# Second part's operand forms ordered behind the first products, forms at both ends of the memory, last third of the norm behind the first column's products

## The chip, the cores and the metric

The kernel runs on one core of one Trainium2 chip. The metric is the device time of one execution in microseconds (us). Before the change it was 2646.94 us, the median of 3 runs (2643.6 to 2652.96). The core has a matrix engine (PE), a vector engine (DVE), an activation engine (ACT), a general engine (POOL), and SP, which here only issues DMAs. Each engine works through its own list of instructions in order; an instruction that waits for a semaphore holds back everything behind it on that engine. PE writes into eight banks of PSUM, each 512 floats wide.

## The reference

One step of a one-layer encoder: a half-step feed-forward layer, a mixer (RWKV-7 heads beside chunk-band attention), a second half-step feed-forward layer and a last norm. The part that matters here:

```
x = x + 0.5 * (silu(rms(x, g1) @ w_gate) * (rms(x, g1) @ w_up)) @ w_down
h = rms(x, g_mix)
proj = h @ w_in                                   # 3328 columns
x = x + concat(rwkv7(proj[:, :1792]), band_attention(proj[:, 1792:])) @ w_out
x = x + 0.5 * (silu(rms(x, g2) @ v_gate) * (rms(x, g2) @ v_up)) @ v_down
y = rms(x, g_final)
```

There are 1024 prompt rows and 8 x 16 sample rows, 1152 tokens in all; the model width is 1024, the feed-forward width 2816. Everything is float32. The change touches no arithmetic: the same products, sums and roundings are made of the same numbers.

## The kernel before

**Precision.** Every matmul operand is held as a pair: `hi`, the number rounded to the engine's fast float32 form (`fp32r`), and `lo`, what the rounding left. A product is three matmuls: hi·hi, hi·lo, lo·hi. So whatever is made for PE is made twice: ACT copies the `hi`, and POOL or DVE subtracts to get the `lo`.

**Tokens and parts.** The 1152 tokens are 9 tiles of 128 rows. In the feed-forward layers they are cut in two parts (`PARTS`): part 0 is tiles 0 to 4, in two halves of 320 tokens, and part 1 is tiles 5 to 8, in two halves of 256.

**Gate and up products.** Each block of 256 feed-forward columns is multiplied in a scheme with seven products in place of eight. For this the activations of a part are turned into seven combinations, the part's *forms* `F`, made by `_x_forms` (L237): for each of four column groups `c`, PE transposes four blocks into PSUM (`ps_n`, L250), ACT copies three of them as `hi` (L260) and DVE makes their `lo` (L261); ACT copies the fourth block into a buffer `bs` (L263), DVE makes four differences there (L262), ACT rounds all four at once (L268) and POOL makes their `lo` at once (L269). The weights get seven forms as well (`_w_forms`: DMA into `raw`, combinations `cmb` on DVE L289, `hi` on ACT L283, `lo` on POOL L284, buffers `frm`). `_gate_up` then runs, for the gate weights and for the up weights, a pass of 7 forms x 2 parts x 12 matmuls = 168 products (L325 to L327) into the tiles `pa` and `pb`, which ACT and DVE empty (`r` L332, `y` L338). There are 11 blocks, so 22 passes in each feed-forward layer.

**Down products.** `_down` reads the hidden values back from memory (`hr`, L398), makes `h` of them (hi on ACT L401, lo on POOL L402), loads and splits two rows of blocks of the down weights (`raw` L380, `spl` L162 on ACT and L163 on POOL), multiplies (`pd`, L418 to L420) and adds to the tiles `x` (L422), 11 times over.

**Mixer.** After the first layer's last down step the norm of the mixer runs in three groups of three tiles (`_norm_t`: `xn` L203, transposes L209, `xg` hi on ACT L211 and lo on DVE L212). Then `_project` loads the old state (`st`, DMA L449, transposed by PE as `ps_st`, L451) and multiplies column by column of `w_in` (`ps_p`, L225 to L227), 24 products for each of the three groups. Near the end the output projection runs tile by tile (`ps_wo`, L1229 to L1231, added to `x` in L1235), and each finished tile is normalised for the second feed-forward layer (L1412 to L1414).

**What sets the order.** The program is written in one order, and a list scheduler puts each engine's instructions in an order of its own that respects data, buffers and the written order as a priority. Buffers come from pools: a pool takes its memory at the left or the right end of SBUF and can only be opened where the memory of closed pools is free; a tag with `bufs=n` has n buffers in turn, and whoever wants the next one waits for its last reader. In the gate and up passes PSUM has two tags of four banks, `a` and `bc`.

Five places are spoken of below, named by letters:

- **A**, the start: norm of the first layer, forms of both parts, first gate pass.
- **B**, the step from the first layer's last up pass to its first down step.
- **C**, the step from its last down step to the first column of `w_in`.
- **D**, the output projection with the second layer's forms and its first gate pass.
- **E**, the step from the second layer's last up pass to its first down step.

Of the kernel before, what the change touches and what calls it, by code (L numbers as in the profile page):

```python
# [16 lines left out]
P = 128  # L17
DM = 1024
# [43 lines left out]
def _bank(k, name):  # L62
    return k.psum.tile([P, 512], F32, tag=k.ptag, name=name)
# [131 lines left out]
def _norm_t(k, v0, rooms):  # L195

    nc = k.nc
    for g in range(3):
        xns = []
        for i in range(3 * g, 3 * g + 3):  # L200
            xn = next(rooms)
            rs = _rms(k, k.x[i], xn)
            nc.vector.tensor_scalar(xn, k.x[i], rs, None, ALU.mult)  # L203
            xns.append(xn)
        hi, lo = _xg_tile(k), _xg_tile(k)
        for c in range(KC):
            ps = k.psum.tile([P, 512], F32, tag="g", name="ps_n")
            for j in range(3):
                nc.tensor.transpose(ps[:, j * P:(j + 1) * P], xns[j][:, c * P:(c + 1) * P], k.ident)  # L209
            gain = k.vec[:, v0 + c:v0 + c + 1]  # L210
            nc.scalar.activation(hi[:, c], ps[:, :TG], AF.Copy, scale=gain)  # L211
            nc.vector.scalar_tensor_tensor(  # L212
                lo[:, c], ps[:, :TG], gain, hi[:, c].bitcast(F32), ALU.mult, ALU.subtract)
        k.xg.append((hi, lo))
        yield
# [19 lines left out]
def _x_forms(k, part, xns):  # L235


    nc = k.nc
    o, n = PARTS[part]
    F = k.F[part]  # L240

    def turned(c, half):
        ps = _bank(k, "ps_n")
        t = o + half * n
        end = t + n
        while t < end:
            i, r = divmod(t, P)
            m = min(P - r, end - t)
            at = t - o - half * n
            nc.tensor.transpose(ps[:, at:at + m], xns[i - o // P][r:r + m, c * P:c * P + P],  # L250
                                k.ident[r:r + m, r:r + m])
            t += m
        return ps[:, :n]

    for c in range(4):
        buf = k.bsp.tile([P, k.bsw], F32, tag=k.bst, bufs=k.nbs, name="bs")
        bs = buf[:, :4 * n].rearrange("p (j n) -> p j n", n=n)
        x11, x12, x21, x22 = [turned(cc, half) for cc, half in ((c, 0), (c, 1), (c + 4, 0), (c + 4, 1))]
        for j, ps in enumerate((x11, x21, x22)):
            nc.scalar.activation(F[:, 0, j, c], ps, AF.Copy)  # L260
            nc.vector.tensor_tensor(F[:, 1, j, c], ps, F[:, 0, j, c].bitcast(F32), ALU.subtract)  # L261
        sub = lambda out, x, y: nc.vector.tensor_tensor(bs[:, out], x, y, ALU.subtract)  # L262
        nc.scalar.activation(bs[:, 2], x12, AF.Copy)  # L263
# [4 lines left out]
        nc.scalar.activation(F[:, 0, 3:7, c], bs, AF.Copy)  # L268
        nc.gpsimd.tensor_tensor(F[:, 1, 3:7, c], bs, F[:, 0, 3:7, c].bitcast(F32), ALU.subtract)  # L269

# [32 lines left out]
def _gate_up(k, wg, wu, hd, m, begun=None):  # L303
# [3 lines left out]
    for up, w in enumerate((wg, wu)):  # L307
        forms = begun if begun and not up else list(_w_forms(k, w[:, 2 * m * P:2 * m * P + 2 * P]))
        state = [{}, {}]
        turns = [(t, p) for t in range(7) for p in range(2)]  # L310
        if m == 0 or (up and m == NF // 2 - 1):
            turns = [(t, p) for p in range(2) for t in range(7)]
        for t, p in turns:
            frm, j, bank = forms[t]
# [3 lines left out]
            if new:  # L318
                ps = k.psum.tile([P, 512], F32, tag="a" if bank == "a" else "bc", bufs=4, name="pa" if bank == "a" else "pb")
                st[bank] = ps[:, :n]  # L320
            ps = st[bank]
            F = k.F[p]
            for c in range(4):
                kw = dict(skip_group_check=True)
                nc.tensor.matmul(ps, frm[:, 0, c], F[:, 0, j, c], start=new and c == 0, stop=False, **kw)  # L325
                nc.tensor.matmul(ps, frm[:, 0, c], F[:, 1, j, c], start=False, stop=False, **kw)  # L326
                nc.tensor.matmul(ps, frm[:, 1, c], F[:, 0, j, c], start=False, stop=c == 3, **kw)  # L327
# [7 lines left out]
            def whole(r, f, half):  # L335
                h = hs[p][:, f, half]
                y = k.hx.tile([P, k.ny], F32, tag="y", bufs=2, name="y")[:, :n]
# [34 lines left out]
def _gate_up_pool(k, s, pool):  # L372
    k.hx = pool(s, "hx")
    k.w = pool(s, "wa")
    k.psum, k.ptag = pool(s, "psum_a", space=PSUM, bufs=4), "a"


def _down_w(k, wd, f, pool, n):
    raw = k.w.tile([P, DM], F32, tag="raw", bufs=k.nraw, name="raw")
    k.nc.sync.dma_start(raw, wd[f * P:(f + 1) * P, :])  # L380
    d = pool.tile([P, 2, DM], F32R, tag="spl", bufs=n, name="spl")
    _split(k, d, raw)
    return d


def _down(k, s, pool, wd, hd, xd, done, beside=(), then=None):


# [3 lines left out]
    w2 = pool(s, "wb")  # L392
    k.h = pool(s, "hb")
    k.xp = pool(s, "xb")
    k.psum, k.ptag = pool(s, "psum_b", space=PSUM, bufs=8), "g"
    for m in range(NF // 2):
        raw = k.h.tile([P, 2, T], F32, tag="hr", bufs=1, name="hr")
        nc.sync.dma_start(raw, hd[m])  # L398
        h = k.h.tile([P, 2, 2, T], F32R, tag="h", bufs=2, name="h")
# [3 lines left out]
        d = [_down_w(k, wd, 2 * m, k.w, 3), _down_w(k, wd, 2 * m + 1, w2, 2)]  # L403
        if m == 0:
            k.x = [k.xp.tile([P, DM], F32, tag=f"x{i}", name="x") for i in range(NT)]
            for i in range(NT):
                nc.sync.dma_start(k.x[i], xd[i])
# [4 lines left out]
        for i in range(NT):  # L412
            a = slice(i * P, (i + 1) * P)
            for n in range(2):
                b = slice(512 * n, 512 * n + 512)
                ps = k.psum.tile([P, 512], F32, tag="g", name="pd")
# [824 lines left out]
def tile_encoder_step(ctx: ExitStack, tc: tile.TileContext, *aps):  # L1241
# [35 lines left out]
    with ExitStack() as s_rw, ExitStack() as s_xg:  # L1277
# [3 lines left out]
        with ExitStack() as s:  # L1281
            fp = [pool(s, f"f{p}") for p in range(2)]
            k.F = [fp[p].tile([P, 2, 7, 4, n], F32R, name="F") for p, (o, n) in enumerate(PARTS)]
            k.ny = 4 * PARTS[0][1]
            _gate_up_pool(k, s, pool)
            k.bsp, k.bst, k.nbs, k.bsw = k.hx, "y", 2, k.ny
            _constants(k, a)
            gain = _gain(k, a["norm_ff1"][0], k.hx, "hs1")
            for p, tiles in enumerate((range(5), range(5, 9))):
                xns = []  # L1290
                for i in tiles:
# [6 lines left out]
                _x_forms(k, p, xns)  # L1298
            for m in range(NF // 2):
                _gate_up(k, w[0], w[1], hd, m)  # L1300
        k.xgp = pool(s_xg, "xg1", "right")
        k.w = pool(s_xg, "w2", "right")
        k.nraw, k.spl = 2, (k.w, 3)
        with ExitStack() as s:
# [3 lines left out]
            def rooms():  # L1308
                t = k.h.tile([P, 2 * 2 * T], F32, tag="h", bufs=2, name="xn")
                for j in range(4):  # L1310
                    yield t[:, j * DM:(j + 1) * DM]
                t = k.h.tile([P, 2 * T], F32, tag="hr", bufs=1, name="xn")
                for j in range(2):
                    yield t[:, j * DM:(j + 1) * DM]
                t = k.h.tile([P, 2 * 2 * T], F32, tag="h", bufs=2, name="xn")
                for j in range(4):
                    yield t[:, j * DM:(j + 1) * DM]

            def done(i):
# [9 lines left out]
            next(norm)  # L1329
            k.first = [_cols(k, a["w_in"][0], c * P) for c in (12, 13)]  # L1330
# [6 lines left out]
        k.psum = pool(s_xg, "psum_g", space=PSUM, side="right", bufs=5)  # L1337
        k.iv = pool(s_xg, "iv", "right")
# [36 lines left out]
    with ExitStack() as s:  # L1375
        fp = [pool(s, "f0")]
        k.F = [fp[0].tile([P, 2, 7, 4, PARTS[0][1]], F32R, name="F")]
        k.hx = pool(s, "hx")
        k.ny = DM
        with ExitStack() as sx:  # L1380
# [4 lines left out]
            k.psum, k.ptag = pool(s_ps, "psum3", space=PSUM, bufs=8), "g"  # L1385
# [14 lines left out]
            for i in range(NT):  # L1400
# [19 lines left out]
            fp.append(pool(s, "f1", "right"))  # L1420
            k.F.append(fp[1].tile([P, 2, 7, 4, PARTS[1][1]], F32R, name="F"))
            k.bsp, k.nbs, k.bsw = pool(s, "bs2", "right"), 2, 4 * PARTS[1][1]
        k.w = pool(s, "wa")
        forms = list(_w_forms(k, w[0][:, 0:2 * P]))
        _x_forms(k, 1, xns[5:])
        s_ps.close()
        k.psum, k.ptag = pool(s, "psum_a", space=PSUM, bufs=4), "a"
        for m in range(NF // 2):
            _gate_up(k, w[0], w[1], hd, m, forms if m == 0 else None)
    with ExitStack() as s:  # L1430
# [9 lines left out]
        k.w = pool(s, "w4")  # L1440
        gp = pool(s, "gain", "right")
# [34 lines left out]
```

## Time and profile before

| what | value |
|---|---|
| median of 3 runs | 2646.94 us |
| the profiled execution's own time | 2648.95 us |
| its span, first to last instruction | 2647.2 us |
| mean granted PE clock | 0.958 |
| DVE busy | 1113.4 us (42%) |
| ACT busy | 900.9 us (34%) |
| POOL busy | 1086.7 us (41%) |
| DMA, mean over the span | 108 GB/s |

The page says how long each engine was busy. The view of waits sums, for each line of the program, the time in which the engine stood still before it and what ended that time. The timeline gives single instructions: start, duration, engine, line, what is written and what is read, how many alike follow each other, and in brackets the idle time before them with its releaser. `SPq` and `ACTq` are DMAs issued from those engines' queues.

### The profile page before, as it was taken

The numbers are of one execution on the slowest core, as the hardware profiler recorded it, in microseconds if no ns is written. First come the engines' busy times: TensorE is split into PE (matmuls) and PEld (weight loads), VectorE is DVE, ScalarE is ACT, GpSimd is POOL, SyncE is SP. The second block draws the span as 40 slices with busy tenths as digits, with TensorE's granted clock in tenths as the row PEclk, the third lists the DMA queues.
The fourth block names the chain that finished last, engine by engine and source line by source line (L and its number), as shares of the span: only waits on it lengthen the run. The fifth ranks groups of instructions, "written<-read, shape, count | busy, mean of one in ns | idle before, by whom it ended". The sixth has DMA issues, their size and how long they took to land. (4 is left out here: it accounts for less than half of the span.)

```text
span 2647.2 us, 43489 instructions
## 1 busy us (share of the span) xinstructions
PE 2429.4 (92%) x17415; PEld 2165.0 (82%) x17415; DVE 1113.4 (42%) x2330; ACT 900.9 (34%) x1903; POOL 1086.7 (41%) x966
## 2 busy tenths in 40 slices
PE   3999999978999899999997999987999999979998
PEld 2999999976888799889875666666999999968886
DVE  5322222213545533856845656344322222225555
ACT  4433333321111443444214667423333333321112
POOL 4645454443443233443224443123554545544341
PEclk9999999998999899999996879988999999989999
DMA  3222112237322223543669983512221122252221
GB/s 111 66 66 84 59 59 84 66 106 243 109 84 68 98 67 125 168 141 113 191 141 205 229 181 99 181 56 72 66 74 62 65 84 66 69 202 81 93 94 72
DMA packets 230283, 284.75 MB, mean 108 GB/s; under 512 B 54920, under 2 KB 183552, under 8 KB 227264
## 3 DMA queue, kind: packets, MB, share of 16 engines
q1 hardware_dynamic: 194044, 226.72, 27.7%
q0 software_dynamic: 7648, 25.43, 4.1%
q10 hardware_dynamic: 28388, 29.81, 3.4%
q8 instruction: 137, 2.24, 0.4%
q14 instruction: 66, 0.54, 0.1%
HBM read 191.79 MB, written 90.12 MB: 106 GB/s over the span
## 5 line engine op out<-in xcount | busy, mean ns | idle before, releaser
L325 PE MATMUL pa<-F,frm 128*128 128x256 f32 (+1 forms) x1408 | 422.3, 300 | 44.6 <-ACT r L332 25.5
L327 PE MATMUL pa<-F,frm 128*128 128x256 f32 (+1 forms) x1408 | 416.8, 296 | 0.0
L326 PE MATMUL pa<-F,frm 128*128 128x256 f32 (+1 forms) x1408 | 416.8, 296 | 0.0
L422 DVE TENSOR_TENSOR x<-pd,x 128x512 f32<-128x512 f32 x396 | 270.3, 689 | 255.3 <-PE pd L420 255.3
L163 POOL TENSOR_TENSOR spl<-raw,spl 128x1024 fp32r<-128x1024 f32 x78 | 187.9, 2411 | 461.9 <-ACT spl L162 461.7
L418 PE MATMUL pd<-spl,h 128*128 128x512 f32 x792 | 314.6, 398 | 33.3 <-ACT spl L162 17.6
L284 POOL TENSOR_TENSOR frm<-cmb,frm 128x512 fp32r<-128x512 f32 x176 | 230.5, 1312 | 219.3 <-ACT frm L283 218.8
L327 PE MATMUL pb<-F,frm 128*128 128x320 f32 (+1 forms) x1056 | 312.7, 296 | 4.0 <-POOL frm L284 4.0
L325 PE MATMUL pb<-F,frm 128*128 128x320 f32 (+1 forms) x1056 | 313.6, 297 | 2.5 <-ACT frm L283 2.5
L326 PE MATMUL pb<-F,frm 128*128 128x320 f32 (+1 forms) x1056 | 312.9, 296 | 2.4 <-POOL F L269 2.4
L420 PE MATMUL pd<-spl,h 128*128 128x512 f32 x792 | 312.2, 394 | 2.5 <-POOL h L402 2.5
L419 PE MATMUL pd<-spl,h 128*128 128x512 f32 x792 | 311.7, 394 | 2.4 <-POOL spl L163 2.4
L325 PEld LDWEIGHTS pa<-F,frm 128*128 128x128 f32 x1408 | 266.8, 189 | 54.1 <-ACT r L332 34.3
L327 PEld LDWEIGHTS pa<-F,frm 128*128 128x128 f32 x1408 | 267.3, 190 | 0.0
L326 PEld LDWEIGHTS pa<-F,frm 128*128 128x128 f32 x1408 | 267.1, 190 | 0.0
L284 POOL TENSOR_TENSOR frm<-raw,frm 128x512 fp32r<-128x512 f32 x132 | 173.9, 1318 | 200.8 <-ACT frm L283 200.8
L162 ACT ACTIVATE spl<-raw 128x1024 fp32r<-128x1024 f32 x78 | 82.2, 1055 | 404.4 <-PE pd L420 341.2
L418 PEld LDWEIGHTS pd<-spl,h 128*128 128x128 f32 x792 | 150.2, 190 | 67.4 <-ACT spl L162 18.5
L327 PEld LDWEIGHTS pb<-F,frm 128*128 128x128 f32 x1056 | 200.5, 190 | 4.5 <-POOL frm L284 4.5
L325 PEld LDWEIGHTS pb<-F,frm 128*128 128x128 f32 x1056 | 200.5, 190 | 2.9 <-ACT frm L283 2.9
L326 PEld LDWEIGHTS pb<-F,frm 128*128 128x128 f32 x1056 | 200.5, 190 | 2.7 <-POOL F L269 2.7
L420 PEld LDWEIGHTS pd<-spl,h 128*128 128x128 f32 x792 | 150.1, 189 | 37.8 <-POOL h L402 3.9
(258 smaller groups left out, 4591.4 us busy)
## 6 DMA issues: line engine op xcount, KB each, us to landing
raw<-in_w_ff_gate_dram SPq DMA_DIRECT2D x22, 1024.0 KB
raw<-in_w_ff_up_dram SPq DMA_DIRECT2D x22, 1024.0 KB, 9.2
raw<-in_w_ff_down_dram SPq DMA_DIRECT2D x44, 512.0 KB, 4.4
raw<-in_w_in_dram SPq DMA_DIRECT2D x26, 512.0 KB, 3.9
hr<-hd SPq DMA_DIRECT2D x11, 1152.0 KB, 5.3
hr<-he SPq DMA_DIRECT2D x11, 1152.0 KB, 5.1
q<-qk POOLq DMA_DIRECT2D x24, 384.0 KB, 9.0
x<-xd SPq DMA_DIRECT2D x18, 512.0 KB, 6.0
```

The lines of the kernel that those rows point to most:

```text
L162: k.nc.scalar.activation(dst[:, 0], raw, AF.Copy)
L163: k.nc.gpsimd.tensor_tensor(dst[:, 1], raw, dst[:, 0].bitcast(F32), ALU.subtract)
L284: nc.gpsimd.tensor_tensor(d[:, 1], x, d[:, 0].bitcast(F32), ALU.subtract)
L325: nc.tensor.matmul(ps, frm[:, 0, c], F[:, 0, j, c], start=new and c == 0, stop=False, **kw)
L326: nc.tensor.matmul(ps, frm[:, 0, c], F[:, 1, j, c], start=False, stop=False, **kw)
L327: nc.tensor.matmul(ps, frm[:, 1, c], F[:, 0, j, c], start=False, stop=c == 3, **kw)
L418: mm(ps, h[:, 0, f, a], d[f][:, 0, b], start=f == 0, stop=False)
L419: mm(ps, h[:, 0, f, a], d[f][:, 1, b], start=False, stop=False)
L420: mm(ps, h[:, 1, f, a], d[f][:, 0, b], start=False, stop=f == 1)
L422: nc.vector.tensor_tensor(xs, ps, xs, ALU.add)
```

## The change

It does seven things.

1. In the gate and up passes the PSUM banks are tagged by part: `a0`, `a1`, `bc0`, `bc1`, two banks each, in place of `a` and `bc` with four each. In the first layer the transposes of part 0's forms use all eight banks, those of part 1 only `a1` and `bc1`.
2. `_x_forms` can be run one column group at a time. A part's forms lie in two tiles, FX (three forms) and FT (four). The `lo` of the first of the four differences moves from POOL to DVE; POOL makes three in one instruction. In the first layer there are three `bs` buffers in place of two.
3. First layer: part 1's norm is written ahead of part 0's forms, and the first `lead=3` weight forms' products of part 0 ahead of part 1's forms. The weight forms of the first pass are made one by one as they are needed.
4. Second layer: part 0's forms are made one column group after each of the output projection's tiles 5 to 8 (before: all at tile 5), and part 1's forms are written behind all seven products of part 0 (`lead=7`).
5. First layer: part 0's FX lies at the right end of the memory, the pools of the down steps (`ha`, `wb`, `hb`, `xb`) are opened in another order, the two `h` buffers lie in two pools, and the loads of the `x` tiles are spread over the first down step.
6. The second layer's down steps have four `spl` buffers in one ring (before three and two in two rings); `h` and `hr` lie where part 0's forms were.
7. The norm of the mixer's third group is written into the last down step as before, but its transposes and `xg` are run from `_mm_cols`, behind the first column's products of groups 0 and 1; the third column's weights are no longer loaded ahead, since their buffer is used for the norm.

On PE at place D, from the products of tile 5 (`ps_wo`) over the transposes of the second layer's forms (`ps_n`) to the first gate product (`pa`), before:

```order
L1231 MATMUL ps_wo<-spl,mx 128x512
L250 MATMUL ps_n<-ident,x 128x128 x2
L250 MATMUL ps_n<-ident,x 128x64 x2
L250 MATMUL ps_n<-ident,x 128x128 x4
...
L250 MATMUL ps_n<-ident,x 128x128 x2
L1229 MATMUL ps_wo<-spl,mx 128x512
...
L1231 MATMUL ps_wo<-spl,mx 128x512
L250 MATMUL ps_n<-ident,x 128x128 x32
L325 MATMUL pa<-F,frm 128x320
```

And in the changed kernel, the transposes after tile 5 and those after the last tile:

```order
L1262 MATMUL ps_wo<-spl,mx 128x512
L251 MATMUL ps_n<-ident,x 128x128 x2
L251 MATMUL ps_n<-ident,x 128x64 x2
L251 MATMUL ps_n<-ident,x 128x128 x4
L251 MATMUL ps_n<-ident,x 128x64 x2
L251 MATMUL ps_n<-ident,x 128x128 x2
L1260 MATMUL ps_wo<-spl,mx 128x512
...
L1262 MATMUL ps_wo<-spl,mx 128x512
...
L251 MATMUL ps_n<-ident,x 128x128 x24
L341 MATMUL pa<-F,frm 128x320
```

Before, all 48 transposes of part 0 stood together, and all 32 of part 1 ahead of the first product. Now 12 stand after each of the tiles 5 to 8, 22 of part 1's 32 stand ahead of the first product, and the last 10 stand between later products.

On PE at place A, around the first gate products (`pb` and `pa`, 320 wide for part 0 and 256 wide for part 1) and the forms' transposes (`ps_n`), before:

```order
L327 MATMUL pb<-F,frm 128x320
L250 MATMUL ps_n<-ident,xn 128x128 x4
L325 MATMUL pb<-F,frm 128x320
L326 MATMUL pb<-F,frm 128x320
L250 MATMUL ps_n<-ident,xn 128x128 x2
L327 MATMUL pb<-F,frm 128x320
L250 MATMUL ps_n<-ident,xn 128x128 x24
L325 MATMUL pa<-F,frm 128x320
```

And after:

```order
L251 MATMUL ps_n<-ident,xn 128x128 x2
L341 MATMUL pa<-F,frm 128x320
...
L343 MATMUL pa<-F,frm 128x320
L251 MATMUL ps_n<-ident,xn 128x128 x8
L341 MATMUL pb<-F,frm 128x320
...
L343 MATMUL pa<-F,frm 128x320
L251 MATMUL ps_n<-ident,xn 128x128 x18
L341 MATMUL pa<-F,frm 128x256
```

Before, the 12 products of one weight form stood among the transposes and all others behind them. Now 36 products of part 0 (three weight forms) stand ahead of most of part 1's transposes.

On SP at place E, the DMAs from the last hidden values written (`he`) to the first loads of the down steps, with the semaphores that each waits for, before:

```order
L361 DMA he_17173<-hs 256x1x512 [waits DMAHW7_49,DVE_49,Pool_49]
L380 DMA raw<-in_w_ff_down_dram 128x1024 [waits PE_49]
L380 DMA raw<-in_w_ff_down_dram 128x1024 [waits DMAHW2_49]
L380 DMA raw<-in_w_ff_down_dram 128x1024 [waits DMAHW3_49,DMAHW0_49,Pool_49]
L380 DMA raw<-in_w_ff_down_dram 128x1024 [waits DMAHW4_49,DMAHW2_49,Pool_49]
L1443 DMA gain<-in_norm_final_dram 128x1024 [waits DMAHW5_49,PE_49]
L407 DMA x<-xd_63 128x1024 [waits DMAHW7_49,DVE_49]
L407 DMA x<-xd_64 128x1024
L398 DMA hr<-he_17164 128x2304 [waits DMAHW1_49]
```

And after:

```order
L377 DMA he_17192<-hs 256x1x512 [waits DMAHW7_49,DVE_49,Pool_49]
L428 DMA hr<-he_17183 128x2304 [waits PE_49]
L401 DMA raw<-in_w_ff_down_dram 128x1024 [waits DMAHW2_49]
L401 DMA raw<-in_w_ff_down_dram 128x1024 [waits DMAHW3_49]
L428 DMA hr<-he_17184 128x2304 [waits DMAHW4_49,DMAHW0_49,Pool_49]
L1493 DMA gain<-in_norm_final_dram 128x1024 [waits DMAHW6_49,PE_49]
L401 DMA raw<-in_w_ff_down_dram 128x1024 [waits DMAHW7_49,DMAHW2_49,Pool_49]
L423 DMA x<-xd_63 128x1024 [waits Pool_49]
```

The first `hr` moved from behind four `raw`, the gain and two `x` to the front, and the `x` tiles moved behind it.

The diff, cut to its core:

```diff
@@ _norm_t @@
             xns.append(xn)
+        yield
         hi, lo = _xg_tile(k), _xg_tile(k)
@@ _x_forms @@
-        nc.scalar.activation(F[:, 0, 3:7, c], bs, AF.Copy)
-        nc.gpsimd.tensor_tensor(F[:, 1, 3:7, c], bs, F[:, 0, 3:7, c].bitcast(F32), ALU.subtract)
+        nc.scalar.activation(FT[:, 0, :, c], bs, AF.Copy)
+        hi = FT[:, 0, :, c].bitcast(F32)
+        nc.vector.tensor_tensor(FT[:, 1, 0, c], bs[:, 0], hi[:, 0], ALU.subtract)
+        nc.gpsimd.tensor_tensor(FT[:, 1, 1:4, c], bs[:, 1:4], hi[:, 1:4], ALU.subtract)
+        yield
@@ _gate_up @@
-        forms = begun if begun and not up else list(_w_forms(k, w[:, 2 * m * P:2 * m * P + 2 * P]))
+        source = _w_forms(k, w[:, 2 * m * P:2 * m * P + 2 * P])
+        forms = [] if m == 0 and not up else list(source)
...
+        if m == 0 and not up:
+            turns = [(t, p) for p in range(2) for t in range(k.lead)]
+            turns += [(t, p) for t in range(k.lead, 7) for p in range(2)]
         for t, p in turns:
+            if m == 0 and not up and (t, p) == (0, 1):
+                between()
+            if t == len(forms):
+                forms.append(next(source))
...
-                ps = k.psum.tile([P, 512], F32, tag="a" if bank == "a" else "bc", bufs=4, name="pa" if bank == "a" else "pb")
+                tag = "a" if bank == "a" else "bc"
+                st[bank] = k.psum.tile([P, 512], F32, tag=f"{tag}{p}", bufs=2, name="pa" if bank == "a" else "pb")[:, :n]
@@ _gate_up_banks (new) @@
+    def turn(part, c):
+        tag = ("a", "bc")[c // 4] + str(1 if part else c % 2)
+        return k.psum.tile([P, 512], F32, tag=tag, bufs=2, name="ps_n")
@@ _down @@
-    w2 = pool(s, "wb")
-    k.h = pool(s, "hb")
+    k.hp = hp = [pool(s, "ha")]
+    k.h = hp[0]
+    if len(k.dspl) == 1:
+        k.dspl.append((pool(s, "wb"), 2))
+    hp.append(pool(s, "hb"))
...
-        h = k.h.tile([P, 2, 2, T], F32R, tag="h", bufs=2, name="h")
+        h = hp[m % 2].tile([P, 2, 2, T], F32R, tag="h", bufs=1, name="h")
...
         for i in range(NT):
+            if m == 0 and i + 2 < NT:
+                x_load(i + 2)
@@ first layer @@
+            k.lead = 3
...
+            xns = norm_part(0)
+            part = _x_forms(k, 0, xns)
+            xns = norm_part(1)
+            for _ in part:
+                pass
             for m in range(NF // 2):
-                _gate_up(k, w[0], w[1], hd, m)
+                _gate_up(k, w[0], w[1], hd, m, lambda: [None for _ in _x_forms(k, 1, xns)])
...
             def done(i):
                 nc.scalar.dma_start(xd[i], k.x[i])
+                if i in (2, 5, 8):
+                    next(norm)
                 if i in (4, 7):
                     next(norm)
...
-            next(norm)
-            k.first = [_cols(k, a["w_in"][0], c * P) for c in (12, 13)]
+            k.norm = norm
@@ second layer @@
-                if i == 5:
-                    _x_forms(k, 0, xns[:5])
+                if i == 4:
+                    part = _x_forms(k, 0, xns[:5])
+                elif i > 4:
+                    next(part)
...
-        forms = list(_w_forms(k, w[0][:, 0:2 * P]))
-        _x_forms(k, 1, xns[5:])
...
+        k.lead = 7
...
         k.w = pool(s, "w4")
+        k.nraw, k.dspl = 2, [(k.w, 4)] * 2
```

More of the change, by code (lines that the diff above doesn't have):

```diff
@@ L204, in _norm_t @@
             xns.append(xn)
+        yield
         hi, lo = _xg_tile(k), _xg_tile(k)
         for c in range(KC):
-            ps = k.psum.tile([P, 512], F32, tag="g", name="ps_n")
+            ps = _bank(k, "ps_n")
             for j in range(3):
@@ L239, in _x_forms @@
     o, n = PARTS[part]
-    F = k.F[part]
+    FX, FT = k.F[part]
     def turned(c, half):
-        ps = _bank(k, "ps_n")
+        ps = k.turn(part, c)
         t = o + half * n
@@ L267, in _x_forms, with _form_tile @@
         sub(3, x21, bs[:, 1])
-        nc.scalar.activation(F[:, 0, 3:7, c], bs, AF.Copy)
-        nc.gpsimd.tensor_tensor(F[:, 1, 3:7, c], bs, F[:, 0, 3:7, c].bitcast(F32), ALU.subtract)
+        nc.scalar.activation(FT[:, 0, :, c], bs, AF.Copy)
[3 more added lines that the diff above has]
+        yield
+def _form_tile(pool, part, forms):
+    return pool.tile([P, 2, forms, 4, PARTS[part][1]], F32R, tag=f"F{forms}", bufs=1, name="F")
 def _w_forms(k, src):
@@ L402, in _down @@
             nc.gpsimd.tensor_tensor(h[:, 1, f], raw[:, f], h[:, 0, f].bitcast(F32), ALU.subtract)
-        d = [_down_w(k, wd, 2 * m, k.w, 3), _down_w(k, wd, 2 * m + 1, w2, 2)]
+        d = [_down_w(k, wd, f) for f in (2 * m, 2 * m + 1)]
         if m == 0:
-            k.x = [k.xp.tile([P, DM], F32, tag=f"x{i}", name="x") for i in range(NT)]
-            for i in range(NT):
-                nc.sync.dma_start(k.x[i], xd[i])
+            for i in range(2):
+                x_load(i)
         if m:
@@ L1280, in tile_encoder_step, with norm_part @@
         w = [a[f"w_ff1_{name}"][0] for name in ("gate", "up", "down")]
[L1281 to L1286, printed above, removed]
+        with ExitStack() as sr, ExitStack() as s:
+            k.F = [(_form_tile(pool(sr, "fx", "right"), 0, 3), _form_tile(pool(s, "ft"), 0, 4))]
+            f1 = pool(s, "f1")
+            k.F.append((_form_tile(f1, 1, 3), _form_tile(f1, 1, 4)))
+            k.ny, k.nyb = 4 * PARTS[0][1], 3
+            k.hx = pool(s, "hx")
+            k.w = pool(s, "wa")
+            k.bsp, k.bst, k.nbs, k.bsw = k.hx, "y", 3, k.ny
+            k.lead = 3
+            _gate_up_banks(k, s, pool)
             _constants(k, a)
             gain = _gain(k, a["norm_ff1"][0], k.hx, "hs1")
-            for p, tiles in enumerate((range(5), range(5, 9))):
+            def norm_part(p):
                 xns = []
-                for i in tiles:
+                for i in (range(5), range(5, 9))[p]:
                     x = k.w.tile([P, DM], F32, tag="frm", bufs=7, name="xn")
@@ L1384, in tile_encoder_step @@
             s_ps = s.enter_context(ExitStack())
-            k.psum, k.ptag = pool(s_ps, "psum3", space=PSUM, bufs=8), "g"
+            k.psum, k.ptag, k.pbufs = pool(s_ps, "psum3", space=PSUM, bufs=8), "g", 8
+            k.turn = lambda part, c: _bank(k, "ps_n")
             s_wx = ExitStack()
```

71 lines of the change are left out of this document (39 added, 32 removed).

## The prediction

> **What bounds the kernel now.** I read the page first, then PE's waits, then the timeline around each place.
>
> ```profile
> PE 2429.4 (92%) x17415; PEld 2165.0 (82%) x17415; DVE 1113.4 (42%) x2330; ACT 900.9 (34%) x1903; POOL 1086.7 (41%) x966
> ```
>
> PE is busy in 92% of the span of 2647.2 us, and but for its own weight loads (PEld), which run beside its products, nothing else is busy in half of it. The products do not change, so the change can only win or lose in PE's idle time, about 218 us.
>
> ```profile
> PE pa L325 <- ACT r L332: 25.5, 39, 1.4
> PE pd L418 <- ACT spl L162: 17.6, 2, 16.9
> PE ps_n L250 <- ACT bs L263: 17.6, 9, 4.5
> PE pa L325 <- DVE bs L262: 14.4, 1, 14.4
> PE pd L418 <- ACT h L401: 13.2, 1, 13.2
> ```
>
> Each row: line that waited, releaser, total us, times, longest. The first is spread over 39 of the 44 gate and up passes, 0.65 us each. The other four sum to 62.8 us and sit at the seams A, B, D and E that the change rewrites. Inside the passes and the down steps the order of each engine stays; a bank of `a0` comes round after two passes, one of `bc0` after one, as the four shared banks did. So I count nothing there, and add up the seams.
>
> **A, the start.** SP loads tiles 7 and 8, ACT copies into `bs`, POOL makes the `lo` of four differences, DVE scales a norm, PE runs the first `pa` and then the first up product:
>
> ```profile
> 35.49 0.34 SPq L1293 DMA_DIRECT2D xn<-in_x_prompt_dram  x1
> ...
> 27.57 0.44 ACT L263 ACTIVATE bs<-ps_n 128x320 f32<-128x320 f32 x1 [3.41 <-POOL F L269]
> ...
> 47.27 2.88 POOL L269 TENSOR_TENSOR F<-bs,F 128x1280 fp32r<-128x1280 f32 x1
> ...
> 57.08 2.57 POOL L269 TENSOR_TENSOR F<-bs,F 128x1024 fp32r<-128x1024 f32 x1 [4.71 <-ACT F L268]
> 62.67 2.57 POOL L269 TENSOR_TENSOR F<-bs,F 128x1024 fp32r<-128x1024 f32 x1 [3.03 <-ACT F L268]
> ...
> 23.11 0.48 DVE L262 TENSOR_TENSOR bs<-bs,ps_n 128x320 f32<-128x320 f32 x1
> 23.51 1.28 DVE L1296 SCALAR_TENSOR_TENSOR xn<-xn,ss,gain 128x1024 f32<-128x1024 f32 x1
> ...
> 47.34 3.90 DVE L1296 SCALAR_TENSOR_TENSOR xn<-xn,ss,gain 128x1024 f32<-128x1024 f32 x1 [0.44 <-POOL ss L187]
> ...
> 66.48 0.61 PE L325 MATMUL pa<-F,frm 128*128 128x320 f32 x1
> ...
> 91.11 0.31 PE L325 MATMUL pa<-F,frm 128*128 128x320 f32 x1
> ```
>
> ACT's copy of a third `bs` waits for POOL, and the copies that would empty PSUM for PE stand behind it. With a third buffer and eight banks this block goes. A column group then costs its busiest engine, DVE: three `lo`, four differences and the new `lo`, about 8 x 0.48 = 3.9 us. I estimate part 0's transposes done at 28 instead of 35.5, when the load of tile 7 was issued. The norms of tiles 7 and 8, done at 47.34 + 3.90 = 51.2, come 10 earlier: 7 from the load, 2.6 from the 3.90 that should be 1.28 with POOL out of its way. Part 1's four groups, at about 3.6 us each, let PE finish its transposes near 55, not 66. The pass took 91.11 - 66.48 = 24.6 us for 168 products, 0.147 each; 36 of them (5.3 us) are now done before, 19.3 remain, about a microsecond more for waits: the up pass starts at 75. **Gain 16**; 11 if part 1's groups keep the 62.67 - 57.08 = 5.6 us, 20 if products fill every gap. What is late next is POOL: seven `lo` of weight forms and the forms' own share one queue.
>
> Against it speaks the Trainium skill ("SBUF — State Buffer", section "SBUF: two separate sides"): DVE with two operands in SBUF and POOL take one pair of ports as an exclusive lock, and the loser blocks for the whole instruction. The trace agrees: the norm at 47.34 took 3.90, the same at 23.51 took 1.28, and the 2.6 between are what POOL's 2.88 from 47.27 had left. By that rule the moved `lo` cannot run beside POOL, and a group gains 2.88/4 - 0.48 = 0.24 instead of 0.72; over eight groups the sum would be 4 us smaller.
>
> **B, into the first down step.** POOL's `lo` of `h` and of the two `spl`, ACT's first split:
>
> ```profile
> 590.53 5.18 POOL L402 TENSOR_TENSOR h<-hr,h 128x1152 fp32r<-128x1152 f32 x2 [4.89 <-ACT h L401]
> ...
> 602.22 2.35 POOL L163 TENSOR_TENSOR spl<-raw,spl 128x1024 fp32r<-128x1024 f32 x1 [2.46 <-ACT spl L162]
> ...
> 596.27 1.06 ACT L162 ACTIVATE spl<-raw 128x1024 fp32r<-128x1024 f32 x1 [4.77 <-DVE room L124]
> ```
>
> On ACT the first split stood behind a DMA that waits for the bias table; now it stands ahead of it. Then POOL runs its two splits right behind `h`: 590.53 + 5.18 + 2 x 2.35 = 600.4 instead of 604.6. **Gain 4**, from 0 to 5. It can be nothing because the two `raw` still stand behind the second `hr` on SP, which waits for POOL; if they land late, the split waits for them instead.
>
> **C, into the projection.** Last `pd`, the first products, the DMA of the state, the last square, and eight transposes of an earlier group:
>
> ```profile
> 886.24 1.09 PE L209 MATMUL ps_n<-ident,xn 128*128 128x128 f32 x8 [0.88 <-DVE xn L203]
> ...
> 890.56 0.39 PE L420 MATMUL pd<-spl,h 128*128 128x512 f32 x1
> ...
> 905.50 0.45 PE L451 MATMUL ps_st<-ident,st 112*128 112x112 f32 x1 [2.87 <-DVE xg L212]
> 905.62 0.67 PE L225 MATMUL ps_p<-xg,spl 128*128 128x384 f32 x1
> ...
> 894.31 0.24 ACT L185 ACTIVATION_READ_ACCUMULATOR xn<-x 128x1 f32 x1
> ...
> 902.67 0.35 ACTq L449 DMA_DIRECT2D st<-in_state_shift_dram  x1
> ```
>
> PE waits from 890.95 to 905.50 with only 24 transposes in it. After, 48 products need nothing of the last group, but `ps_st` stands before them, and its DMA on ACT behind the last square: 894.5 plus the 2.8 us that it took from 902.67 to 905.50 gives 897.4. So products start 8.1 earlier; then 24 transposes (24 x 1.09/8 = 3.3) and about a microsecond of the evictions come between them and the rest. **Gain 4**, from 2 to 8. Columns 1 and 2 have their weights; the third's load, now later, is wanted 25 us later.
>
> **D, output projection and second forms.** The start of the transposes behind tile 5's products, the first product behind them, the last tile's end, first gate product, first up product; the last norm on DVE, and ACT's `bs`:
>
> ```profile
> 1753.86 3.34 PE L250 MATMUL ps_n<-ident,x 128*128 128x128 f32 x24
> ...
> 1773.75 0.80 PE L1229 MATMUL ps_wo<-spl,mx 128*128 128x512 f32 x1 [4.49 <-ACT bs L263]
> ...
> 1809.26 1.47 PE L250 MATMUL ps_n<-ident,x 128*128 128x128 f32 x12
> ...
> 1835.08 0.61 PE L325 MATMUL pa<-F,frm 128*128 128x320 f32 x1 [14.45 <-DVE bs L262]
> ...
> 1860.57 0.31 PE L325 MATMUL pa<-F,frm 128*128 128x320 f32 x1
> ...
> 1814.14 1.28 DVE L1414 SCALAR_TENSOR_TENSOR x<-x,ss,gain 128x1024 f32<-128x1024 f32 x1 [1.65 <-DMA xd<-x]
> ...
> 1765.66 0.44 ACT L263 ACTIVATE bs<-ps_n 128x320 f32<-128x320 f32 x1 [2.67 <-POOL F L269]
> ```
>
> PE made no product from 1753.86 to 1773.75, 19.9 us, because three of the four groups, some 7 us each, went one after another through one `bs` before the last transposes could run. After, one group lies beside each tile of about 11 us of products ((1809.26 - 1773.75)/3, less the cold start), so only the transposes of three groups stay: 36 at 3.34/24 = 0.14, 5 us. Products that start cold go as well, 2 us (0.80 in the row at 1773.75 where C's warm one of the same width took 0.39). So 19.9 - 5 + 2 = 17: the projection ends at 1809.3 - 17 = 1792. The last tile's norm ended 6.2 behind it (1814.14 + 1.28), so at 1798.5; part 1's first two groups and half of the third stand ahead of the first `pa`, and the third's copy needs a `bs` that POOL frees when the first group is done, about 8 us after its first transpose; with the copies and transposes behind that, `pa` starts at about 1810 instead of 1835. Part 1's last groups and the weights' 14 forms still go through POOL, so I give 2 of the 25 back. **Gain 23**, from 17 (only the stop goes) to 27.
>
> **E, into the second layer's down step.** SP's `raw` and first `hr`, the usual landing time of `hr`, PE's first products, POOL:
>
> ```profile
> 2336.18 10.58 SPq L380 DMA_DIRECT2D raw<-in_w_ff_down_dram  x4
> ...
> 2348.24 0.55 SPq L398 DMA_DIRECT2D hr<-he  x1
> ```
>
> ```profile
> hr<-he SPq DMA_DIRECT2D x11, 1152.0 KB, 5.1
> ```
>
> ```profile
> 2359.57 0.80 PE L418 MATMUL pd<-spl,h 128*128 128x512 f32 x1 [13.17 <-ACT h L401]
> ...
> 2364.91 0.79 PE L420 MATMUL pd<-spl,h 128*128 128x512 f32 x1 [0.94 <-POOL h L402]
> ```
>
> `hr` is issued at 2336.2 and lands at 2341.5 or a little later; one copy of ACT later POOL does two `lo` of `h` (5.2 by B's row), three small products (2.1) and two splits (4.7), ending near 2354. PE runs on from there, not from 2364.9. **Gain 10**, 7 to 13. The `x` tiles come later, but eight banks hold the sums of four tiles meanwhile.
>
> **Sum.** 16 + 4 + 4 + 23 + 10 = 57, so the profiled execution's 2648.95 becomes 2592. It lies 2.0 above the median; against the median I say **2590**. Bounds: 37 to 73, that is 2574 to 2610.
>
> **Rivals.** *Half the gain.* Forms beside products make each other slow:
>
> ```profile
> L289 DVE TENSOR_TENSOR cmb<-raw x88: 674/693/2827, 31.0 to 2302.0; 128x512 f32<-128x512 f32 x88
> ```
>
> A combination takes 0.69 in the median and 2.83 beside POOL, at D. If the first passes then wait form by form, A gives 5 and D only its stop, 17; with 8 for the rest the time is 2617. For it: POOL's queue; against: the passes have 24 us for seven forms.
>
> *Slower.* The second layer's down steps lose a fifth of their split buffers. The waits there:
>
> ```profile
> POOL spl L163 <- ACT spl L162: 112.0, 8, 14.5
> ```
>
> POOL is idle for 14 us in each of 8 steps, so a later release is hidden. Only if a step's splits came over 14 us later would PE wait; from 57/9 = 6.3 us beyond that in each of nine steps the gain is gone, and if the chain of two splits and `h` (10 us) lay wholly bare, the time is 2590 + 90 = 2680. Against it: four buffers are still two steps.
>
> *More.* E's and C's waits vanish nearly whole and A and D reach their tops: 20 + 5 + 12 + 27 + 18 = 82, time 2565. Against: the DMAs above.
>
> *It does not do what it says*: the scheduler's order makes the moved products wait at the head of PE for forms as late as before. The order shown speaks against it, except at B.
>
> **How the numbers follow.** Forecast 0.66, half 0.20, more 0.08, slower 0.03, nothing 0.03. The range, 2570 to 2622, holds the forecast's bounds and the half case; "more" and the last two lie outside. 0.3% is 8 us, about what a measurement can tell from no change: faster 0.94, same 0.03, slower 0.03.
>
> **What would show it.** A: the first up product at 75, no `bs` wait of ACT on POOL. B: last split at 600. C: `ps_st` 6.5 us behind the last `pd`, not 14.5. D: no stop inside the output projection, and the first `pa` 17 or 18 us behind its end, not 26. E: `hr` first at the seam, and 8 us from the last `pa` to steady `pd`, not 19. I am wrong if the waits inside the passes or the down steps grow, or if D's first pass has stops for forms.

## The result, and the profile after

The changed kernel takes 2608.48 us, the median of 4 runs (2605.25 to 2609.70); the kernel before took 2649.36 beside it. The ratio is 0.9846, with a 95% interval from 0.9824 to 0.9868. The change gains 41 us, faster as forecast and inside the range of 2570 to 2622, but 18 us short of the forecast 2590. The profiled execution took 2605.25 us, 43.7 less than the one before. Of the four runs of the kernel with seven `lo` on DVE, further down, one took 4615.6 us; its 2597.98 is the median of all four, and the other three alone give 2596.60.

Both traces cut at the same instructions show where those 43.7 us come from. All lengths are in us, between starts on PE, worked out from the timelines; the predicted gain is that of the prediction's sum.

| stretch | before | after | gain | predicted |
|---|---|---|---|---|
| A: start to first up product | 91.1 | 87.0 | 4.1 | 16 |
| first layer's other passes | 489.1 | 487.7 | 1.4 | 0 |
| B: last `pa` to steady `pd` | 24.4 | 20.4 | 4.0 | 4 |
| first down steps | 285.9 | 286.6 | -0.7 | 0 |
| C: last `pd` to the first `ps_g` | 94.7 | 88.5 | 6.2 | 4 |
| mixer to the last `ps_wo` | 823.7 | 805.2 | 18.5 | 17 |
| D, rest: last `ps_wo` to first up product | 51.6 | 51.2 | 0.4 | 6 |
| second layer's other passes | 485.5 | 484.1 | 1.4 | 0 |
| E: last `pa` to steady `pd` | 18.8 | 8.9 | 9.9 | 10 |
| second down steps | 270.0 | 271.5 | -1.5 | 0 |

(`ps_g`, in the mixer, is the first product of another kind behind the columns of `w_in`.) Of the 18.5 in the mixer's stretch, 16.1 lie between the first and the last product of the output projection (129.5 before, 113.4 after). Four terms came out near their predicted size. Two did not: A gave a quarter, and the second half of D nothing.

PE's waits in the changed kernel (line that waited, releaser, total us, times, longest):

```profile
PE pa L341 <- ACT r L348: 25.2, 37, 1.6
PE ps_n L251 <- DVE xn L1332: 15.7, 6, 10.5
PE pd L450 <- POOL spl L163: 13.3, 5, 5.4
PE pd L449 <- ACT spl L162: 12.1, 1, 12.1
PE ps_n L251 <- ACT bs L264: 8.8, 6, 3.2
```

The waits inside the passes stay (25.2 here, 25.5 before), so the PSUM banks tagged by part cost nothing there. The waits of 14.4 and 13.2 for `bs` and `h` are gone. At B and E PE now waits for splits.

**Where the forecast held.** At B, POOL's `lo` of `h` and both splits now follow without a gap, and PE runs on:

```profile
585.14 5.20 POOL L432 TENSOR_TENSOR h<-hr,h 128x1152 fp32r<-128x1152 f32 x2 [5.07 <-ACT h L431]
590.31 4.71 POOL L163 TENSOR_TENSOR spl<-raw,spl 128x1024 fp32r<-128x1024 f32 x2
...
595.07 0.79 PE L450 MATMUL pd<-spl,h 128*128 128x512 f32 x1 [0.67 <-POOL spl L163]
```

The splits end at 595.02, 9.9 behind the start of `h` against 14.0 before (604.57 - 590.53): the 4 us of the sum.

At E, `hr` is SP's first DMA at the seam, and PE's last wait ends 8.9 behind the last `pa`:

```profile
2301.17 0.34 SPq L428 DMA_DIRECT2D hr<-he  x1
...
2316.59 0.79 PE L450 MATMUL pd<-spl,h 128*128 128x512 f32 x1 [5.41 <-POOL spl L163]
2319.59 0.80 PE L450 MATMUL pd<-spl,h 128*128 128x512 f32 x1 [1.35 <-POOL spl L163]
```

At C the state's DMA is issued as the last square starts (884.27 on ACT), and `ps_st` comes 2.6 later, 5.2 behind the last `pd` (6.5 was forecast, 14.9 before):

```profile
884.32 0.38 ACTq L480 DMA_DIRECT2D st<-in_state_shift_dram  x1
...
886.92 0.42 PE L482 MATMUL ps_st<-ident,st 112*128 112x112 f32 x1 [4.83 <-DMA st<-in_state_shift_dram]
```

In the output projection each column group's 12 transposes take 1.75 us between the products of two tiles, and PE does not stop:

```profile
1737.28 1.75 PE L251 MATMUL ps_n<-ident,x 128*128 128x128 f32 x12
1750.06 1.75 PE L251 MATMUL ps_n<-ident,x 128*128 128x128 f32 x12
1762.84 1.75 PE L251 MATMUL ps_n<-ident,x 128*128 128x128 f32 x12
1775.62 2.08 PE L251 MATMUL ps_n<-ident,x 128*128 128x128 f32 x15
```

**Where it failed.** PE at A: the last of the first 36 products, part 1's transposes, two waits, two products behind them, and the first up product:

```profile
45.27 0.64 PE L341 MATMUL pb<-F,frm 128*128 128x320 f32 x1 [1.25 <-ACT frm L291]
...
49.04 0.64 PE L343 MATMUL pb<-F,frm 128*128 128x320 f32 x1 [2.33 <-POOL frm L292]
...
53.56 1.40 PE L251 MATMUL ps_n<-ident,xn 128*128 128x128 f32 x8
...
62.51 0.42 PE L251 MATMUL ps_n<-ident,xn 128*128 128x128 f32 x2
...
72.48 0.39 PE L342 MATMUL pb<-F,frm 128*128 128x256 f32 x1 [3.06 <-DVE F L271]
74.15 0.58 PE L342 MATMUL pa<-F,frm 128*128 128x256 f32 x1 [1.13 <-POOL F L272]
...
75.60 0.47 PE L341 MATMUL pa<-F,frm 128*128 128x320 f32 x1
75.86 0.47 PE L342 MATMUL pa<-F,frm 128*128 128x320 f32 x1
...
87.00 0.31 PE L341 MATMUL pa<-F,frm 128*128 128x320 f32 x1
```

The 24 products from 45.27 took 8.3 us and stood ahead of part 1's next transposes, at 53.56. One of them waited 2.33 for POOL's `lo` of its weight form; most of the others followed each other 0.27 apart, where a running pass has 0.147. The transposes ended at 62.9, not near 55, and the pass needed 24 more, not 20.

At D, the view of stretches (us long, then the busy time and instructions of PE, PEld, DVE, ACT and POOL, the granted PE clock, DMA share and rate): the gate pass before, and the same pass after.

```profile
1835.10:1860.60 25.50, 24.32 (x169) 24.12 (x170) 5.44 (x9) 10.62 (x20) 11.90 (x8) 0.92 0.14 42
```

```profile
1791.30:1826.60 35.30, 28.29 (x180) 26.73 (x180) 22.34 (x33) 17.73 (x35) 26.15 (x16) 0.89 0.10 31
```

The first gate product came 10 us sooner behind the projection (15.9 instead of 26.1), and the pass took 10 us longer (35.3 instead of 25.5). DVE and POOL, which before had done most of the forms when the pass began, were busy for 22 and 26 us of it. The forms had only been moved into the pass. PE stands still for 7.0 us in it, against 1.2 before: 3.3 for `y` on DVE and 1.6 for `r` on ACT, which empty the banks, and 2.2 for forms and `bs`.

### The profile page after: what moved, and what is told of

It reads as the page before. It is cut to its first block, busy times and chain, and to the rows that moved or that the text cites. A ratio compares the mean times of both kernels' runs of the same rounds, so it can differ in the third digit from the quotient of the medians.

```text
span 2603.5 us, 43481 instructions
## 1 busy us (share of the span) xinstructions
PE 2422.6 (93%) x17415; PEld 2161.5 (83%) x17415; DVE 1124.8 (43%) x2346; ACT 899.8 (35%) x1903; POOL 1076.5 (41%) x966
## 4 chain that ended last, share of the span: by engine, by line
PE 42%; DVE 5%; POOL 3%; issue 3%; ACT 2%; DMA 2%; ACTq 0%; POOLq 0%; DVEq 0%
PE pa L341 3%; PE pd L450 3%; PE pd L451 3%; PE pd L449 3%; PE pa L343 3%; PE pa L342 3%; PE pb L341 2%; PE pb L342 2%; PE pb L343 2%; POOL frm L292 2%; PE ps_s L1132 1%; PE ps_o L1186 1%; PE ps_pt L1171 1%; PE ps_yc L975 1%; PE ps_wo L1261 1%
## 5 line engine op out<-in xcount | busy, mean ns | idle before, releaser
L341 PE MATMUL pa<-F,frm 128*128 128x256 f32 (+1 forms) x1408 | 424.6, 302 | 34.7 <-ACT r L348 25.2
```

What stands on the lines that cost most here:

```text
L341: nc.tensor.matmul(ps, frm[:, 0, c], F[:, 0, jj, c], start=new and c == 0, stop=False, **kw)
```

## The experiments

Theory: at A and D the vector work on forms (DVE, ACT, POOL) sets when the gate pass ends, whatever PE is given first. Rivals: the products ahead of the forms do hide time, and something else took it back; or they push the forms back and do harm. For every kernel I give the time and, from its one profiled execution, the two lengths A (start to first up product; 91.1 before, 87.0 after) and D (last `ps_wo` to first up product; 51.6 and 51.2). Kernels whose edit did not touch A still gave 86.2 to 87.4 there, so differences of a microsecond mean nothing.

**Order of products and forms.** In the second layer:

```diff
+        for _ in _x_forms(k, 1, xns[5:]):
+            pass
         for m in range(NF // 2):
-            _gate_up(k, w[0], w[1], hd, m, lambda: [None for _ in _x_forms(k, 1, xns[5:])])
+            _gate_up(k, w[0], w[1], hd, m, lambda: None)
```

> The changed kernel, but in the second layer part 1's forms are written ahead of all gate products, as before the change. Place D, last product of the output projection to first up product: 51.5 us before, 51.0 changed, though the first gate product came 10 us sooner. Theory 'the forms set the end': vector work on DVE, ACT and POOL decides when the gate pass ends, whatever PE does first: D stays at 49 to 53, the time within 3 us of 2608. Rival 'products hidden, loss elsewhere': D rises to 57 or more, the time to 2614 or more. Third: products ahead of the transposes push the forms back: D falls to 47 or less, the time to 2604 or less.

Measured: 2609.42 us, D 49.7. And the same edit in the first layer:

> The changed kernel, but in the first layer part 1's forms are written ahead of the gate products of part 0. Place A, first up product: 91.1 before, 87.0 changed. Theory 'the forms set the end': 84 to 89, the time within 3 us of 2608. Rival 'products hidden, loss elsewhere': 91 or later, the time 2612 or more. Third: products ahead of the transposes push part 1's forms back: 83 or sooner, the time 2604 or less.

Measured: 2608.01 us, A 84.4. The edit that stands first in the title, in either layer, is worth nothing in the time. With the order undone, A is 2.6 us shorter and D 1.5, the second hardly more than scatter. The theory held, with a touch of the third reading.

**Part 0's forms over the projection's tiles.**

```diff
-                if i == 4:
-                    part = _x_forms(k, 0, xns[:5])
-                elif i > 4:
-                    next(part)
+                if i == 5:
+                    for _ in _x_forms(k, 0, xns[:5]):
+                        pass
```

> The changed kernel, but the second layer's part 0 forms are made all at tile 5 of the output projection, as before. First to last product of the output projection: 129.5 us before, 113.4 changed. Theory: the stop inside the projection comes back whole, 128 to 130, and since nothing behind it depends on it the time rises by 15 to 17, to 2623 to 2626. Rival 'the stop is only moved': part 1's forms then start with less in front of them, the stretch behind the projection shrinks by 5 or more, and the time rises by 10 or less.

Measured: 2622.35 us, 14 more than the changed kernel, just under what was expected. First to last product of the projection took 127.0, and PE stands as before. Its timeline, from the transposes to the next product of the projection:

```profile
1743.38 3.33 PE L251 MATMUL ps_n<-ident,x 128*128 128x128 f32 x24
...
1755.53 3.11 PE L251 MATMUL ps_n<-ident,x 128*128 128x128 f32 x12 [4.13 <-ACT bs L264]
1762.76 0.80 PE L1260 MATMUL ps_wo<-spl,mx 128*128 128x512 f32 x1 [4.12 <-ACT bs L264]
```

19.4 us without a product, as 19.9 before. D shrank to 48.0, so some 3 of the stop are made up behind the projection; the rest is the interleaving's own, a third of the whole gain.

**The third norm group ahead of the projection again.**

```diff
+            next(norm)
             k.norm = norm
```

> The changed kernel, but the mixer's third norm group is transposed and evicted ahead of the projection, as before. Place C, from the last down product to the first product of the output's next stage (ps_g): 94.7 us before, 88.5 changed. Theory: the 48 products of the first column hide it; back to 94 to 96, the time 5 to 7 longer, 2613 to 2616. Rival 'the down steps' other memory gained it': 88 to 90, the time unchanged.

Measured: 2610.31 us, and 90.2 in C against 88.5: only 1.7 of C's 6.2 come back, so the expected 5 to 7 were wrong. The rival's 88 to 90 is closer, but this kernel does not test the cause that it named. The trace shows where most of the rest lies: from the last `pd` to `ps_st` this kernel takes 11.3 us, the kernel before 14.9. One line that became faster there is the scaling of `xn` on DVE (count, shortest/median/longest in ns), in the kernel before and in this one:

```profile
L203 DVE TENSOR_SCALAR xn<-x,ss x9: 752/755/2681, 865.0 to 897.7; 128x1024 f32<-128x1024 f32 x9
```

```profile
L203 DVE TENSOR_SCALAR xn<-x,ss x9: 752/753/782, 859.6 to 889.6; 128x1024 f32<-128x1024 f32 x9
```

Before, the third column's weights were split in the middle of the last norms (POOL busy with them for 2.51 from 893.88), and POOL set constants right behind; two scalings took 3.51 together and one 2.30. In this kernel the three take 2.36 in all, 3.4 less. It is likely that giving that load up, a side effect of the change's memory plan, cleared them, but no kernel tried the load alone.

**DVE's share of the `lo`.**

```diff
-        nc.vector.tensor_tensor(FT[:, 1, 0, c], bs[:, 0], hi[:, 0], ALU.subtract)
-        nc.gpsimd.tensor_tensor(FT[:, 1, 1:4, c], bs[:, 1:4], hi[:, 1:4], ALU.subtract)
+        nc.gpsimd.tensor_tensor(FT[:, 1, :, c], bs, hi, ALU.subtract)
```

> The changed kernel with one part undone: POOL again makes the lo of all four differences in one instruction, DVE none. Landmarks of the changed kernel: first up product at 87.0 us (place A), and 51.0 us from the last product of the output projection to the first up product of the second layer (place D). Theory 'one port': DVE's small lo could not run beside POOL and only took a place in DVE's queue, so A stays at 85 to 88, D at 49 to 52, the time within 4 us of 2608. Rival 'POOL is the bound': a fourth more work on POOL for eight column groups costs A 3 to 6 and D 2 to 4, the time is 2613 to 2618.

Measured: 2609.33 us, A 84.4, D 49.1. Moving that `lo` to DVE gained nothing. A fell by 2.6 without it: the wait of 3.06 for `DVE F` at 72.48 above is that `lo`, which on DVE stood behind two combinations of 1.67 and 1.75. Without it PE's last wait at A, for POOL's `lo`, ends at 72.20 and not at 74.15.

**Which engine?** Three kernels change the load of one engine in the first gate pass. DVE makes the `lo` of the seven weight forms; POOL makes it twice; DVE makes each combination three times.

```diff
-        nc.gpsimd.tensor_tensor(d[:, 1], x, d[:, 0].bitcast(F32), ALU.subtract)
+        (nc.vector if first else nc.gpsimd).tensor_tensor(d[:, 1], x, d[:, 0].bitcast(F32), ALU.subtract)
```

> The changed kernel, but in the first gate pass of each layer DVE makes the lo of the seven weight forms (about 0.69 us each) and not POOL (1.27). Places A (first up product at 87.0) and D (51.2 from the last product of the output projection to the first up product). Theory 'the port that DVE and POOL share is the bound': 7 x 0.58 = 4 us less use of it, A and D fall by 2 to 5 each. Rival 'POOL's queue is the bound': 9 us less on POOL, they fall by 6 to 9. Rival 'DVE's queue is the bound': 5 us more on DVE, they rise by 3 to 5.

```diff
+        for _ in range(2 if first else 1):
+            nc.gpsimd.tensor_tensor(d[:, 1], x, d[:, 0].bitcast(F32), ALU.subtract)
```

> The changed kernel, but in the first gate pass of each layer POOL makes the lo of each weight form twice, 7 x 1.27 = 9 us more on POOL and on the port. Port or POOL as the bound: A (87.0) and D (51.2) grow by 6 to 9 each. Rival 'PE, cold clock and waits in its own order are the bound, POOL has slack': they grow by 0 to 3.

```diff
+        for _ in range(3 if first else 1):
+            nc.vector.tensor_tensor(d, x, y, op)
```

> The changed kernel, but in the first gate pass of each layer DVE makes each of the four weight combinations three times, 8 x 0.69 = 5.5 us more on DVE and on the port, nothing on POOL. Port or DVE as the bound: A (87.0) and D (51.2) grow by 4 to 6 each. POOL's queue alone as the bound: 0 to 2.

| kernel | time | A | D |
|---|---|---|---|
| changed | 2608.48 | 87.0 | 51.2 |
| seven `lo` from POOL to DVE | 2597.98 | 79.5 | 48.4 |
| seven more `lo` on POOL | 2624.54 (one run) | 93.6 | 60.3 |
| eight more combinations on DVE | 2605.69 (one run) | 85.3 | 52.0 |

A ends with a stretch in which PE waits for nobody, and its pace there differs between the kernels, so the end of PE's last wait at A is a cleaner mark. In the changed kernel it is 74.15 (shown above). With seven `lo` on DVE, with seven more on POOL and with eight more combinations, that wait and the next products of 320 columns stand at:

```profile
68.80 0.38 PE L342 MATMUL pb<-F,frm 128*128 128x256 f32 x1 [1.44 <-DVE F L271]
...
69.97 0.31 PE L341 MATMUL pa<-F,frm 128*128 128x320 f32 x1
70.12 0.31 PE L342 MATMUL pa<-F,frm 128*128 128x320 f32 x1
```

```profile
80.34 0.58 PE L343 MATMUL pa<-F,frm 128*128 128x256 f32 x1 [1.05 <-POOL F L272]
...
82.43 0.47 PE L342 MATMUL pa<-F,frm 128*128 128x320 f32 x1
82.70 0.47 PE L343 MATMUL pa<-F,frm 128*128 128x320 f32 x1
```

```profile
74.51 0.39 PE L343 MATMUL pb<-F,frm 128*128 128x256 f32 x1 [0.98 <-DVE F L271]
...
75.45 0.31 PE L342 MATMUL pa<-F,frm 128*128 128x320 f32 x1
75.60 0.31 PE L343 MATMUL pa<-F,frm 128*128 128x320 f32 x1
```

These products start 0.26 to 0.27 apart in the changed kernel and the second of these, 0.15 in the first and the third. So of the 7.5 that the first gains at A, 5.4 lie ahead of the mark and about 2 in the pace behind it; the 1.7 that the third seems to gain is pace alone.

POOL's 9 us more cost 6.6 at A and 9.1 at D. DVE's 5.5 us more cost 0.4 at A's last wait and 0.8 at D, though they use the operands' port as well. So neither DVE's queue nor the port that both share is the bound: the path goes through POOL's `lo` of the weight forms. PE's waits at D in the kernel with seven more:

```profile
PE pa L344 <- POOL frm L293: 5.0, 3, 2.3
...
PE pb L344 <- POOL frm L293: 2.1, 1, 2.1
```

where the changed kernel's same stretch has a single wait of 0.6 for `frm`. Relieving POOL brought 7.5 at A, as expected of its queue, but only 2.8 at D, which is no more than the port theory expected; at D it is the combinations' 0.8 that speaks against the port.

**How far it goes.** DVE makes the `lo` in the first up pass as well:

```diff
-        source = _w_forms(k, w[:, 2 * m * P:2 * m * P + 2 * P], m == 0 and not up)
+        source = _w_forms(k, w[:, 2 * m * P:2 * m * P + 2 * P], m == 0)
```

> The changed kernel with DVE making the lo of the weight forms in the first gate pass and in the first up pass of each layer, 14 instead of e8's 7. Theory 'POOL's queue' as the only bound: A and D fall again by 2 to 6 against e8 (79.5 and 48.4), time 2587 to 2594. Theory 'POOL's queue, then DVE's': DVE, which also empties PSUM, is now the one that is late: A and D, or the up pass behind them, gain nothing or lose 1 to 4, time 2597 to 2604.

Measured: 2592.27 us (2589.55 to 2594.79), ratio to the kernel before 0.9787, interval 0.9769 to 0.9805; A 77.5, D 47.1. The changed kernel's interval, 0.9824 to 0.9868, lies wholly above this one, so this version beats both kernels, by 57 and 16 us. The time fits POOL alone better than the fuller DVE that I expected. But the gate pass at D in it:

```profile
1780.80:1811.80 31.00, 27.12 (x179) 26.00 (x179) 22.11 (x43) 17.09 (x34) 6.24 (x3) 0.90 0.11 35
```

POOL is down from 26 to 6 us there, and the pass still takes 31.0 where the 168 products took 25.5 before. Below 47 something else holds D.

Three more kernels asked what, with edits shown above. Seven `lo` on DVE, with the forms ahead of the products:

> The changed kernel with DVE making the lo of the first gate pass's weight forms in each layer (as in e8_lo_on_dve, 2598) and, in both layers, part 1's forms written ahead of the gate products. Theory 'POOL's queue, then DVE's': with POOL relieved, products ahead of the forms have nothing to hide, so the order again matters little: A 77 to 80 (e8: 79.5), D 46 to 49 (e8: 48.4), time 2594 to 2599. Rival 'products ahead pay once POOL is free': A 82 or later, D 51 or more, time 2602 or more.

Measured: 2596.40 us, A 80.7, D 46.0, near the 2597.98 without it. Then the version with 14 `lo` on DVE, with the small `lo` of the token forms back on POOL, and the same with the forms first:

> The kernel of e12_dve_both (DVE makes the lo of 14 weight forms in each layer; A 77.5, D 47.1, 2592) with POOL making the lo of all four differences of the token forms again, DVE none, as in e1_pool_lo. Theory 'POOL first, then DVE': DVE is now the fuller one, the small lo leaves it at a price of 0.4 on POOL: A and D fall by 1 to 4 each, time 2586 to 2591. Rival 'POOL still the bound': A and D rise by 1 to 3, time 2594 to 2598.

Measured: 2593.70 us, A 78.6, D 45.3, between the theory's time and the rival's.

> The kernel of e13_split with part 1's forms written ahead of the gate products in both layers. Theory 'the forms set the end, PE's order does not': A and D within 2 of e13's, time within 4 of it. Rival 'with the vector engines relieved, products ahead of the forms hide time': A or D at least 4 longer than e13's, time 5 or more above it.

Measured: 2592.58 us, A 75.7, D 46.0. A fell by 2.9, more than the 2 that the theory allowed; the time stayed. Neither time differs from 2592.27 by more than the runs scatter. So the order of products and forms matters no more with POOL relieved than without. What holds D at 45 to 47 stays open: POOL's queue and the small `lo` are ruled out, and of the copies on ACT and the emptying of PSUM on DVE none was tried alone. Nor was what the trace with 14 `lo` on DVE shows ahead of its first `pa`: PE waits 3.7 for the last tile's norm and 4.7 for `bs`, and some 20 first products of the pass start 0.27 apart.

## Why the prediction was right or wrong

**Bound and seams: right.** The waits inside the passes stayed, and the gain came from the five seams.

**B, E and the projection's stop: right in mechanism and size** (4 for 4.0, 10 for 9.9, 17 for 16.1 within the projection). Each was a sum of durations from rows along one queue: the splits behind `h` on POOL, the DMA of `hr` at the head of SP, the transposes left between the projection's products. The kernel with all forms at tile 5 shows the last; B and E rest on their rows, as no kernel undid them alone.

**C: right in sum, off in cause.** 4 was predicted and 6.2 came. I put it all down to the 48 products; they are worth 1.7. The rest I had listed only as harmless ("the third's load, now later, is wanted 25 us later"): the trace puts the larger part in the last norms, whose scalings took 3.4 less once that load was gone.

**A: the term was mis-sized, 16 for 4.1.** The steps up to the norms were right: tile 7's load was issued at 29.7 (28 forecast), the last norm ended at 41.9 (51.2 - 10 forecast). Two steps behind them failed. "Part 1's four groups, at about 3.6 us each, let PE finish its transposes near 55": they ended at 62.9, and at 61.1 even with no product written ahead of them, so the order is the smaller part of these 8 us. "36 of them (5.3 us) are now done before": I priced 36 products at the 0.147 of a pass that had all its weight forms. The 24 from 45.27 took 0.35 each, with a wait for a form and mostly at 0.27 apart, and what was left of the pass behind the transposes took 24.1 us where 20 was forecast. "What is late next is POOL" was said, but given no price. It had one: seven `lo` less on POOL bring A to 79.5. With 14 less A is 75.7 to 78.6, D 45.3 to 47.1 and the time 2592 to 2594, close to the 75, the 45.6 (51.6 - 6) and the 2590 of the forecast. So the price of POOL's `lo` of the weight forms is of the size of what was missed, although those kernels also relieve POOL in the first up pass.

**D's second half: 6 for 0.4.** The step that failed is "I give 2 of the 25 back". The first `pa` did come early, 15.9 behind the projection (17 or 18 forecast), and 10 were given back in a pass with stops for forms, which the prediction had named as a sign of being wrong; with the forms written first again D is no longer (49.7), so the early products bought nothing. At A and D it is the rival "half the gain" that came true, in mechanism and in size: 5 for 4.1, and 17 for the 18.9 of both halves of D. It fell short only in the rest, 8 for 20.1. The 41 gained lie between its 30 and the forecast's 57, nearer to the rival's; that the time lies in the range is due to the range's having been drawn around both.

**The port rule: fits rows, sets no length.** The rule of the Trainium skill ("SBUF — State Buffer", section "SBUF: two separate sides") that the loser blocks for the whole instruction fits again: a norm at A took 3.26 beside POOL, 1.28 alone. In this row the time lost, 1.98, is 0.2 less than what POOL's instruction had left (36.10 + 2.25 - 36.18 = 2.17); in the prediction's row it is 2.62 of 2.81. With it the forecast would have been 4 us nearer. But it does not set the length of A or D: 5.5 us more use of the port by DVE put PE's last wait at A only 0.4 later.

**Slower rival: did not occur.** With four split buffers, POOL still idles 14.4 at most ahead of a split in the second down steps, and they took 271.5 instead of 270.0.

## What to carry to other kernels

Work that is moved ahead of a wait only gains if what follows the wait is not made by the same queue; price the moved products at the pace at which their operands are made, not at the pace of a pass that has them ready. Test a moved order by undoing the order alone: here the first edit of the title was worth nothing, and the interleaving beside full products (14 us) and a DMA put at the head of its queue (10 us at its seam, not undone alone) were worth most. Look at the spacing of the products before reading a difference of 2 us: sixteen products at 0.27 instead of 0.147 make as much. When two engines can do the same small operation, count it first on the one that the chain passes through: 14 subtractions taken from POOL in each layer brought 16 us more.

## What the runs showed of the hardware

DVE's and POOL's subtractions over the same 128x512 operands cost 0.69 and 1.27 us each when undisturbed, and a combination on DVE that met POOL took 1.75 or so, 1.06 more, a little less than one POOL instruction. I had expected this sharing to set the length of the form-making stretches. It did not: eight more combinations on DVE per layer moved PE's last wait at A by +0.4 and D by +0.8, while seven more `lo` on POOL moved them by +6.2 and +9.1. Early products are not free either: those that followed a wait at A came 0.27 apart and not 0.147.
